# Small last blocks, loops over a place's blocks, and an earlier small-block table in the MoE section of a one-core kernel

## The chip, the cores and the metric

The kernel runs on one core of a Trainium2 chip. The metric is the time of one execution on the device in microseconds (us); lower is better. A core has TensorE (PE, matrix products; loading of the stationary operand is shown apart as PEld), VectorE (DVE), ScalarE (ACT), GpSimd (POOL) and the queue engine SyncE (SP), which here starts the large transfers. Each engine works through its own list of instructions in order and waits for others through semaphores. Matrix products collect in PSUM, whose banks DVE and ACT read.

## The reference

One layer: a mixer (HGRN2 heads and a convolution), a norm, then a mixture of 16 SwiGLU experts with two experts for each of 512 tokens, and a norm. The part around the change is the mixture:

```python
s = jax.nn.sigmoid((t @ router_w).astype(jnp.float32))       # 512 tokens x 16 experts
...
_, idx = lax.top_k(jnp.where(in_group, sb, -jnp.inf), TOP_K)  # best 2 in the best group
...
for e in range(N_EXPERTS):
    h = jax.nn.silu(t @ w_gate[e]) * (t @ w_up[e])            # 1024 -> 512
    y = y + combine[:, e:e + 1] * (h @ w_down[e])             # 512 -> 1024
```

How many tokens an expert gets is known only on the chip. The router's tables are worked out there: for each expert how many tokens it has, and for each row of work which token it takes and with which weight.

## The kernel before, in words

The execution has three parts: the mixer (up to about 322 us), a prologue that works out the router's tables and the first block, and a section written by hand (`moe`, from about 353 us), in which each engine has a program of its own with loops, branches on registers and semaphores.

**Places and blocks.** The experts are worked through in 16 "places": the first three are experts 0, 1 and 2, whose weights are loaded early; the others follow by their number of tokens in a fixed pattern. With the reference's inputs the places hold 9 (raised to 33), 42, 23, 1, 343, 49, 16, 38, 15, 257, 12, 31, 165, 22, 1 and 0 tokens. A place is cut into blocks of up to 64 rows, 26 in all. A **large** block takes 64 rows by 512 columns in two column groups of PE; a **small** one, for a place of at most 32 rows, takes 32 rows by 256 columns in four, with half the time on PE. Before, a place is small or large as a whole. Places 2, 3, 6, 8, 10, 11, 13 and 14 are small.

**Weights.** SP keeps a ring of weights for three places: eight tiles of gate and up, four of down. PE's `mark("fg", 8)` tells SP that a place's gate and up tiles have all been used and may be loaded over, `mark("fd", 4)` the same for down. SP then starts the transfers for the place three further on, and each pair of tiles raises a semaphore `full_g`, the down tiles `full_d`.

**One block in the section.** PE waits for `e` (a buffer is free) and `x` (the block's rows, turned and modulated, are in XT). It does the gate and up products of the eight chunks k = 0 to 7 (`up`, L501), with two transposes of the block before between k = 3 and 4 (`turn`, L599). Then it transposes the rows of the next block (`turned_rows`, L492), waits for `h`, and does the down product of the block **before** (`down`, L510). Meanwhile ACT applies Silu (L692) and copies the gathered rows (L685); DVE copies the turned hidden rows (L719, which gives `h`), multiplies (L724), modulates the next block's rows into XT (L727 and L729, which gives `x`) and evicts the product with its weights (L739). POOL gathers rows by index (L487) and adds results into DRAM (L832). Which size DVE and POOL use for a block is read from a table `cnt` (columns 64 on) which `small` fills.

**A place on PE.** `place(x)` does the first block (`block_`, of the size of the place, with waits for the weights), then `finish(x - 1)`, the down product of the last block of the place before, then marks `fd`, and then `rest`, a loop over the blocks from the second on, all large. Then it marks `fg`. The section begins with two register loads of counts (`load`), `rest(0)`, and then a loop of 15 places, three in a turn.

**The prologue.** `tables` (L293 on) works out indices and weights between the chunks of the first block's up product (`between(i)` issues the chunks that `todo[i]` lists). `small` (L220) comes behind the first block's Silu (L531) and multiplication (L532); then the second block's rows are turned and modulated (L346, L347). The first block's results sit in two banks of their own (`pg`, `pt`). Two ACT operations (L525) write ones into the banks `pz[0]` and `pz[1]` beforehand, and a dummy Silu (L527) asks for the Silu's table early. The order in which instructions stand on an engine here is set by a scheduler from their dependences.

Line 1002 in the profile is a helper that records all operations of the mixer. Line 103 is the router's first step on DVE; L131 and L158 are matmuls of its choice of experts and of the gathering of the first rows.

Of the kernel before, what the change touches and what calls it, by code (L numbers as in the profile page):

```python
# [85 lines left out]
class Router:  # L86
# [85 lines left out]
    def order(self, bank):  # L172
# [44 lines left out]
        self.bs, self.nrows = work.tile([16, 1]), rows  # L217
        v.tensor_copy(self.bs, ps[0:16, 80:81])

    def small(self, bank):  # L220
# [7 lines left out]
        v.tensor_scalar(at, K.iotab[:16, :], self.bs, sm[:, 1:2], op0=OP.is_equal, op1=OP.mult)  # L228
        ps = bank()
        nc.tensor.matmul(ps[0:1, 0:32], K.onesb[:16, 0:1], at, start=True, stop=True, skip_group_check=True)  # L230
        v.tensor_copy(K.cnt[:, 64:96], ps[0:1, 0:32])
# [60 lines left out]
    def tables(self, bank, between):  # L292
# [5 lines left out]
        pi, p32 = pb[:, 0:32], pb[:, 32:64]  # L298
# [21 lines left out]
    def weight_tables(self, bank, between):  # L320
# [11 lines left out]
        between(1)  # L332
# [5 lines left out]
        between(2)  # L338
# [130 lines left out]
def moe(nc, tc, K, ctx, work, W, n2d, zd, out):  # L469
# [11 lines left out]
    pg = psum.tile([128, 2, 256], F32, name="pg", bufs=1)  # L481
    pt = psum.tile([128, 4, 2, 64], F32, name="pt", bufs=1)
# [32 lines left out]
    todo = {0: (0, 1, 2, 3, 4, 5), 1: (6,), 2: (7,)}  # L515
# [5 lines left out]
    bank = lambda: psum.tile([128, 512], F32, name="tbl", bufs=2)  # L521
    with tc.manual_schedule():

        for p in (pz[0][:, 0, :], pz[1][:, 0, :]):
            s.activation(p.rearrange("p (a n) -> p a n", a=4), K.onesb[:, None, :].to_broadcast([128, 4, 128]), AF.Copy)  # L525
# [7 lines left out]
        K.router.small(bank)  # L533
        turned_rows()
        modulate(v, K, st.XT, pt)
# [3 lines left out]
    pg = pz[2][:, 0, :].rearrange("p (u n) -> p u n", u=2)  # L539
    pt = pz[2][:, 1, :].rearrange("p (c h r) -> p c h r", c=4, h=2)  # L540
    ph, po = pz[3][:, 0, :], pz[3][:, 1, :]
# [43 lines left out]
    with tc.tile_critical():  # L585
        with nc.Block() as block:  # L586
            @block.tensor
            def _(pe):
                pe.sem_inc(sem["e"], 1)
                pe.sem_inc(sem["x"], 1)  # L590
# [11 lines left out]
                def block_(x, n, fresh, nxt=None):  # L602

                    for k in range(8):
                        if k == 4:
                            turn()
                        if fresh and k % 2 == 0:
                            wait(pe, full_g[x % 3][k // 2], 64)
                        if k == 6 and nxt:
                            nxt()  # L610
# [13 lines left out]
                def rest(x):  # L624

                    with pe.If_lt(rows[x % 3], 65):
                        pass
                    with pe.Else():
                        with pe.Fori(64, rows[x % 3], 64):
                            take(pe, "e")  # L630
                            take(pe, "x")
                            block_(x, 2, False)
                            take(pe, "h")
                            product(x, 2)
                    mark("fg", 8)

                def by_rows(x, f):
                    with pe.If_lt(rows[x % 3], 33):
                        f(1)
                    with pe.Else():  # L640
                        f(2)

                def finish(x):
                    take(pe, "h")
                    by_rows(x, lambda n: product(x, n))

                def place(x, nxt):

                    take(pe, "e")
                    take(pe, "x")  # L650
                    by_rows(x, lambda n: block_(x, n, True, nxt))
                    finish(x - 1)
# [1362 lines left out]
```

## Time and profile before

| what | value |
|---|---|
| median of 3 runs | 672.32 us (672.11 to 676.18) |
| the profiled execution's own time | 670.53 us |
| its span in the trace | 668.7 us |
| mean granted clock of TensorE | 0.930 of full speed |
| PE busy | 576.2 us, 86% of the span |
| DVE / ACT / POOL busy | 343.1 / 168.1 / 254.3 us |
| moved by DMA | 170.66 MB, mean 255 GB/s |

The profile is one execution. A row of a timeline gives the start in us from the span's beginning, the length in us, the engine, the line of the code, the operation, the tiles written and read, and how many instructions the row holds; a bracket at its end gives the idle time of the engine just before, and what ended it ("PEq L554" is PE's own sequencer waiting for a semaphore in the section). [...] The DMA share is the mean busy share of the core's 16 DMA engines.

### The profile page before, as it was taken

To read this page: it belongs to the slowest core of one execution; us is meant where nothing else is said; L and a number is where in the kernel's file an instruction comes from. 1 tells how busy PE (TensorE), PEld (TensorE's weight loads), DVE (VectorE), ACT (ScalarE), POOL (GpSimd) and SP (SyncE) were. 2 spreads that over 40 slices of the span, in tenths; PEclk is the share of its full clock that TensorE was granted. 3 is DMA by queue.
4 is the path that set the end of the run, shared out by engine and by line. 5 is a ranking of instruction groups with operands and counts; after the bars stand their busy time and mean duration, and the time that the engine had idled before them with its cause. 6 is when DMAs were issued, how large, how long until landed. Compare 5 with 4: busy or idle time off the path is not lost. (4 is left out here: it accounts for less than half of the span.)

```text
span 668.7 us, 10479 instructions
## 1 busy us (share of the span) xinstructions
PE 576.2 (86%) x3499; PEld 313.9 (47%) x3500; DVE 343.1 (51%) x693; ACT 168.1 (25%) x256; POOL 254.3 (38%) x209
## 2 busy tenths in 40 slices
PE   4899999897997968996776979999976999999970
PEld 2577878565665535774432423333332333433430
DVE  6547596999669774788651312231321222322355
ACT  1443468534411233318110000000100101101112
POOL 2235594977921332647202222213221121331315
PEclk9999999897778978997977989999989999999976
DMA  8963322696336778739985999924999995799943
GB/s 293 353 209 98 97 91 67 218 306 243 92 117 217 255 275 303 256 136 395 378 259 193 368 375 390 374 69 117 374 376 383 387 383 163 250 377 376 319 148 126
DMA packets 78783, 170.66 MB, mean 255 GB/s; under 512 B 8866, under 2 KB 18031, under 8 KB 78718
## 3 DMA queue, kind: packets, MB, share of 16 engines
q1 hardware_dynamic: 69456, 149.19, 62.3%
q0 software_dynamic: 9136, 20.80, 11.4%
q8 instruction: 21, 0.34, 0.2%
q14 instruction: 28, 0.23, 0.1%
q10 hardware_dynamic: 142, 0.09, 0.0%
HBM read 154.96 MB, written 15.34 MB: 255 GB/s over the span
## 5 line engine op out<-in xcount | busy, mean ns | idle before, releaser
L832 POOL DMA_INDIRECT zd<-flat,dst x25 | 39.9, 1596 | 203.0 <-POOLq L554 189.1
L501 PE MATMUL pz<-wt,flat 128*32 128x256 f32 (+1 forms) x672 | 93.1, 490 | 5.7 <-PEq L554 5.7
L1002 POOL TENSOR_TENSOR wL<-w,wH 128x1024 fp32r<-128x1024 f32 x30 | 73.9, 2466 | 55.2 <-ACT wH L1002 55.1
L510 PE MATMUL pz<-wt,flat 128*64 128x512 f32 (+1 forms) x544 | 83.8, 513 | 3.1 <-PEq L554 2.0
L1002 PE MATMUL pj<-U,wH 128*128 128x512 f32 x256 | 80.6, 394 | 4.2 <-DVE U L1002 3.2
L1002 PE MATMUL pj<-wH,U 128*128 128x512 f32 x224 | 77.1, 416 | 7.0 <-DVE q L1002 4.6
L501 PE MATMUL pz<-R,flat 128*64 128x512 f32 (+1 forms) x384 | 67.9, 534 | 6.8 <-PEq L554 6.8
L692 ACT ACTIVATE flat<-pz 128x256 f32<-128x256 f32 x25 | 9.6, 383 | 238.6 <-ACTq L554 238.6
L1002 DVE SCALAR_TENSOR_TENSOR mx<-R,convw,mx 128x512 f32<-128x512 f32 x88 | 66.4, 754 | 3.4 <-DVEq L1891 0.6
L1002 PEld LDWEIGHTS pj<-wH,U 128*128 128x128 f32 x224 | 44.5, 199 | 26.7 <-issue 13.1
L501 PEld LDWEIGHTS pz<-wt,flat 128*32 128x32 f32 (+1 forms) x672 | 32.6, 124 | 50.2 <-issue 44.8
L724 DVE TENSOR_TENSOR flat<-pz,flat 128x256 f32<-128x256 f32 x25 | 10.6, 424 | 88.2 <-DVEq L554 82.2
L1002 PEld LDWEIGHTS pj<-U,wH 128*128 128x128 f32 x256 | 47.5, 188 | 16.7 <-DVE U L1002 4.4
L719 DVE COPY flat<-pz 128x256 f32<-128x256 f32 x26 | 11.0, 424 | 80.6 <-DVEq L554 72.3
L1002 PE MATMUL pj<-U,wL 128*128 128x512 f32 x128 | 49.9, 390 | 0.0
L510 PEld LDWEIGHTS pz<-wt,flat 128*64 128x64 f32 (+1 forms) x544 | 27.4, 128 | 44.5 <-issue 40.9
L1002 PE MATMUL pj<-wL,U 128*128 128x512 f32 x112 | 45.6, 407 | 0.0
L487 POOL DMA_INDIRECT flat<-n2d,idx_i x28 | 27.8, 991 | 42.4 <-issue 23.2
L501 PEld LDWEIGHTS pz<-R,flat 128*64 128x64 f32 (+1 forms) x384 | 22.3, 129 | 41.2 <-issue 39.3
L1002 POOL TENSOR_TENSOR R<-R 128x512 f32<-128x512 f32 x28 | 39.3, 1408 | 4.6 <-ACT R L1002 3.3
L1002 ACT ACTIVATE wH<-w 128x1024 fp32r<-128x1024 f32 x30 | 31.5, 1054 | 26.9 <-PE pj L1002 13.7
L739 DVE SCALAR_TENSOR_TENSOR flat<-pz,X,g2h 128x512 f32<-128x512 f32 x18 | 13.5, 751 | 38.5 <-DVEq L554 38.5
(394 smaller groups left out, 805.2 us busy)
## 6 DMA issues: line engine op xcount, KB each, us to landing
wt<-in_w_down_dram SPq DMA_DIRECT2D x60, 512.0 KB, 10.6
wt<-in_w_gate_dram SPq DMA_DIRECT2D x80, 256.0 KB
wt<-in_w_up_dram SPq DMA_DIRECT2D x80, 256.0 KB, 8.6
q<-in_ada_w_dram SPq DMA_DIRECT2D x28, 512.0 KB, 8.3
w<-in_w_in_dram SPq DMA_DIRECT2D x24, 512.0 KB, 3.8
aw<-in_ada_w_dram SPq DMA_DIRECT2D x20, 512.0 KB, 7.1
R<-in_w_gate_dram SPq DMA_DIRECT2D x40, 256.0 KB, 5.6
R<-in_w_up_dram SPq DMA_DIRECT2D x40, 256.0 KB, 7.9
```

The source lines that it names most:

```text
L487: return g.indirect_dma_start(out=to, out_offset=None, in_=n2h, in_offset=bass.IndirectOffsetOnAxis(ap=K.idx[:, i:i + 1], axis=0))
L501: i = eng.matmul(pg[m * j:m * j + m, :, 0:cw], xT[:, c, h, 0:m], w[:, :, cw * j:cw * j + cw], start=k == 0, stop=k == 7)
L510: i = eng.matmul(po[m * q:m * q + m, 0:dw], st.hT[:, c * 128 + j * m:c * 128 + j * m + m], W.dn(x, f)[:, dw * q:dw * q + dw], start=f == 0 ...
L692: s.activation(st.SL, pg[:, 0, :], AF.Silu).then_inc(sem["s"], 1)
L719: v.tensor_copy(st.hT, ph[:, 0:256]).then_inc(sem["h"], 1)
L724: v.tensor_tensor(st.HB, pg[:, 1, :], st.SL, op=OP.mult).then_inc(sem["e"], 1)
L739: v.scalar_tensor_tensor(st.o[j % 3][:, :256 * n], po[:, :256 * n], w[:, j:j + 1], g2, op0=OP.mult, op1=OP.mult).then_inc(sem["o"], 1)
L832: g.indirect_dma_start(out=zd.rearrange("r (q c) -> (r q) c", c=dw), out_offset=bass.IndirectOffsetOnAxis(ap=dst[:, j:j + 1], axis=0), in_ ...
L1002: return f(out, *a, **k)
```

## The change

1. `small` marks the **last block of each place** small if at most 32 rows are left in it, whatever the place's size. It moves from behind the first block's multiplication into `tables`, between the first two and the next four chunks of the first up product, and the matmuls that gather the tokens of 32-row blocks (L309) move ahead of the first chunks, into a bank of their own.
2. The second block's rows are modulated inside the section, as DVE's first work there, and PE no longer counts `x` up itself.
3. `pg`, `pt`, `ph` and `po` lie in the two last pairs of banks from the start; the two fills with ones (L525) are gone.
4. On PE a place is one loop over its blocks. In each turn a compare chooses a small or a large block, a second one whether the product is that of a block of the same place or the last one of the place before (`finish`, by a register `left` that holds how many rows were left). The waits for the gate and up tiles no longer count down; `done` does that, once a place, ahead of the mark `fg`. A third register load stands at the section's start.

With the inputs above the places whose last block becomes small are 4 (343 rows, the sixth block has 23) and 9 (257 rows, the fifth has 1).

The diff, cut to its core:

```diff
     def small(self, ps):
-        v.tensor_scalar(sm[:, 0:1], self.nrows, 0.0, None, op0=OP.is_gt)
-        v.scalar_tensor_tensor(sm[:, 1:2], self.nrows, 32.0, sm[:, 0:1], op0=OP.is_le, op1=OP.mult)
+        v.scalar_tensor_tensor(sm[:, 0:1], self.bs, 64.0, self.nb, op0=OP.subtract, op1=OP.add)
+        v.tensor_tensor(sm[:, 1:2], self.nrows, self.nb, op=OP.subtract)
+        v.tensor_scalar(sm[:, 1:2], sm[:, 1:2], -32.0, None, op0=OP.is_le)
...
+        v.tensor_scalar(at, K.iotab[:16, :], sm[:, 0:1], sm[:, 1:2], op0=OP.is_equal, op1=OP.mult)
+        nc.tensor.matmul(ps, K.onesb[:16, 0:1], at, start=True, stop=True, skip_group_check=True)
+        v.tensor_copy(K.cnt[:, 64:96], ps)
...
+        pb2 = bank()
+        pi, p32 = pb[:, 0:32], pb2[:, 32:64]
...
-        between(0)
         for i in range(8):
             for q in range(4):
                 nc.tensor.matmul(p32[32 * q:32 * q + 32, :], toks[:, i, 0:32], K.st.ones[:, i], start=i == 0, stop=i == 7,
                                  skip_group_check=True)
+        between(0)
+        self.small(pb2[0:1, 64:96])
+        between(1)
         self.weights()
...
-    todo = {0: (0, 1, 2, 3, 4, 5), 1: (6,), 2: (7,)}
+    todo = {0: (0, 1), 1: (2, 3, 4, 5), 2: (6,), 3: (7,)}
...
-        for p in (pz[0][:, 0, :], pz[1][:, 0, :]):
-            s.activation(p.rearrange("p (a n) -> p a n", a=4), K.onesb[:, None, :].to_broadcast([128, 4, 128]), AF.Copy)
         s.activation(st.SL[:, 0:1], K.rexp[:, 0:1], AF.Silu)
...
-        K.router.small(bank)
         turned_rows()
-        modulate(v, K, st.XT, pt)
...
+                def finish(x):
+                    take(pe, "h")
+                    with pe.If_lt(left, 33):
+                        product(x, 1)
+                    with pe.Else():
+                        product(x, 2)
+                def blocks_(x, first, nxt=None):
+                    n = rows[x % 3]
+                    with pe.Fori(first, n, 64) as at:
+                        take(pe, "e")
+                        take(pe, "x")
+                        with pe.If_lt(n, at + 33):
+                            block_(x, 1)
+                        with pe.Else():
+                            block_(x, 2)
...
+                            with pe.If(at > 0):
+                                again()
+                            with pe.Else():
+                                finish(x - 1)
+                                mark("fd", 4)
+                                wait(pe, full_d[x % 3], 64)
+                                nxt()
+                        pe.reg_alu(left, n, at, OP.subtract)
+                def done(x):
+                    for k in range(4):
+                        pe.sem_inc(full_g[x % 3][k], -64)
+                    mark("fg", 8)
...
+                pe.reg_load(left, K.cnt[0:1, 0:1])
...
+                modulated()
...
-                    for k in range(4 if i else 0):
+                    for k in range(4):
```

The places below are those at which the order of instructions on an engine differs. A row is a line, an operation, tiles, and a shape or a count.

**ACT, from the mixer's tail to the first block's Silu, before.** `X` and `q` are tiles of the norm that ends the mixer, `sg` are the router's sigmoids.

```order
L1002 ACTIVATE X<-X,zmv 128x1024
L1002 ACTIVATE q_84<-X,zmv 128x1024
...
L1002 ACTIVATE flat<-pj,cc 128x128 x2
L1002 ACTIVATE sg<-pj 128x16 x4
L165 ACTIVATE flat<-pj 128x512
L525 ACTIVATE pz_3142<-onesb 128x512
L525 ACTIVATE pz_3143<-onesb 128x512
L527 ACT_TABLE_LOAD
L527 ACTIVATE flat<-rexp 128x1
...
L531 ACTIVATE flat<-pg 128x256
```

The same stretch of ACT in the changed kernel (line 1020 is the helper's new number):

```order
L1020 ACTIVATE X<-X,zmv 128x1024
L528 ACT_TABLE_LOAD
L528 ACTIVATE flat<-rexp 128x1
L1020 ACTIVATE q_84<-X,zmv 128x1024
...
L1020 ACTIVATE flat<-pj,cc 128x128 x2
L1020 ACT_TABLE_LOAD
L1020 ACTIVATE sg<-pj 128x16 x4
L165 ACTIVATE flat<-pj 128x512
...
L532 ACT_TABLE_LOAD
L532 ACTIVATE flat<-pz_3142 128x256
```

The dummy Silu with its table load has moved up, behind the first `X` activation of the norm; the sigmoids and the first block's Silu each have a table load directly ahead of them, and the two fills are gone.

**DVE, the end of the prologue and the section's start, before.** The branches are the entry into the section.

```order
L331 COPY flat<-tbl 64x32
L532 TENSOR_TENSOR flat<-pg,flat 128x256
L225 TENSOR_SCALAR flat<-flat 16x1
L226 SCALAR_TENSOR_TENSOR flat<-flat 16x1
L228 TENSOR_SCALAR flat<-iotab,flat 16x32
L231 CAST cnt_i<-tbl 1x32
L346 TENSOR_TENSOR flat<-pt,scT 128x512
L347 TENSOR_TENSOR flat<-flat,shT 128x512
L2010 UNCONDITIONAL_BRANCH
L715 UNCONDITIONAL_BRANCH
```

The same stretch of DVE in the changed kernel:

```order
L334 COPY flat<-tbl 64x32
L533 TENSOR_TENSOR flat<-pz_3142,flat 128x256
L2028 UNCONDITIONAL_BRANCH
L728 UNCONDITIONAL_BRANCH
L731 TENSOR_TENSOR flat<-pz_3143,scT 128x512
L733 TENSOR_TENSOR flat<-flat,shT 128x512
L557 TENSOR_LOAD cnt_i
```

The four operations of `small` have left the prologue's end, and the two of the modulation stand behind the entry.

**PE, the end of a place's turn in the changed kernel.** L514 are down products, L614 are marks; the first compare chooses between a further block of the place and `finish`, the second the size of the last product of the place before.

```order
L635 UNCONDITIONAL_BRANCH
L644 COMPARE_AND_BRANCH
L514 MATMUL pz_3143<-wt_3080,flat 64x512 x2
...
L644 UNCONDITIONAL_BRANCH
L622 COMPARE_AND_BRANCH
L514 MATMUL pz_3143<-wt_3067,flat 32x256 x4
...
L614 MATMUL pz_3142<-onesb 32x1
L590 ISA
L590 TENSOR_LOAD cnt_i
L646 UNCONDITIONAL_BRANCH
L651 ISA
L630 COMPARE_AND_BRANCH
L614 MATMUL pz_3142<-onesb 32x1
```

Before, PE has there, for the loop over a place's blocks from the second on:

```order
L510 MATMUL pz_3143<-wt_3080,flat 64x512 x2
L510 MATMUL pz_3143<-wt_3081,flat 64x512 x2
L510 MATMUL pz_3143<-wt_3077,flat 64x512 x2
L510 MATMUL pz_3143<-wt_3078,flat 64x512 x2
L629 REGISTER_ALU
L629 COMPARE_AND_BRANCH
L628 UNCONDITIONAL_BRANCH
L621 MATMUL pz_3143<-onesb 32x1
```

Behind the product of a block two compares and the register load now stand, where only the loop's own compare stood.

## Rows read from the trace of the kernel before

**Rows 1.** Windows: busy us (instructions) by engine, granted clock, DMA share, GB/s.
```profile
440.00:461.00 21.00, 21.00 (x101) 6.85 (x96) 5.02 (x9) 2.03 (x4) 5.17 (x4) 1.00 0.27 50
491.00:524.00 33.00, 23.68 (x169) 8.97 (x164) 5.90 (x11) 2.03 (x4) 5.17 (x4) 0.84 1.05 388
...
570.00:635.00 65.00, 63.63 (x567) 26.34 (x565) 19.69 (x35) 7.09 (x14) 18.08 (x14) 1.00 0.98 339
...
637.00:638.00 1.00, 0.36 (x4) 0.21 (x8) 0.42 (x2) 0.00 (x0) 1.00 (x1) 0.50 0.00 0
```

**Rows 2.** Timeline of PE (start, length, line, tiles, count): place 4's last block.
```profile
449.27 3.60 PE L501 MATMUL pz<-wt,flat 128*64 128x512 f32 x16
...
457.34 3.65 PE L510 MATMUL pz<-wt,flat 128*64 128x512 f32 x16
```

**Rows 3.** Timeline of PE: blocks of places 9 to 12.
```profile
575.00 3.65 PE L510 MATMUL pz<-wt,flat 128*64 128x512 f32 x16
...
578.59 0.42 PE L501 MATMUL pz<-wt,flat 128*32 128x256 f32 x3
...
583.29 1.93 PE L510 MATMUL pz<-wt,flat 128*32 128x256 f32 x32
...
586.18 3.65 PE L501 MATMUL pz<-R,flat 128*64 128x512 f32 x16 [0.95 <-PEq L554]
...
596.45 3.65 PE L501 MATMUL pz<-R,flat 128*64 128x512 f32 x16 [0.21 <-PEq L554]
```

**Rows 4.** Timeline of DVE: the rows for place 12's first and second block.
```profile
584.92 0.69 DVE L729 TENSOR_TENSOR flat<-flat,shT 128x512 f32<-128x512 f32 x1
...
595.61 0.69 DVE L729 TENSOR_TENSOR flat<-flat,shT 128x512 f32<-128x512 f32 x1
```

**Rows 5.** Timeline of ACT, from the mixer's tail to the section.
```profile
302.47 1.28 ACT L1002 ACT_TABLE_LOAD   x1
303.76 0.20 ACT L1002 ACTIVATE early<-early 128x1 f32<-128x1 f32 x1
...
321.70 0.82 ACT L1002 ACTIVATE sg<-pj 128x16 f32<-128x16 f32 x4
...
338.28 1.28 ACT L527 ACT_TABLE_LOAD   x1
...
349.58 0.38 ACT L531 ACTIVATE flat<-pg 128x256 f32<-128x256 f32 x1 [0.76 <-PE pg L501]
```

**Rows 6.** Timeline of DVE, from the mixer's tail to the section.
```profile
315.82 0.81 DVE L1002 TENSOR_SCALAR q<-X,zmv 128x1024 f32<-128x1024 f32 x1
...
322.55 0.23 DVE L103 TENSOR_TENSOR flat<-sg,rbias 128x64 f32<-128x64 f32 x1 [1.73 <-ACT sg L1002]
...
350.00 0.42 DVE L532 TENSOR_TENSOR flat<-pg,flat 128x256 f32<-128x256 f32 x1 [2.31 <-ACT flat L531]
...
352.55 0.69 DVE L347 TENSOR_TENSOR flat<-flat,shT 128x512 f32<-128x512 f32 x1
```

**Rows 7.** Timeline of POOL in the mixer's tail.
```profile
314.97 0.19 POOL L1002 TENSOR_TENSOR zmv<-zmv 128x1 f32<-128x1 f32 x1
```

**Rows 8.** Timeline of PE, from the router to the section's first mark.
```profile
322.15 2.75 PE L1002 MATMUL pa<-onesb 128*128 128x512 bf16 x12
325.85 0.20 PE L131 MATMUL pj<-flat,tri 128*128 128x64 bf16 x1 [0.95 <-DVE flat L125]
...
327.31 1.94 PE L158 MATMUL pj<-q,flat 128*64 128x512 f32 x8 [0.92 <-DVE flat L152]
...
337.89 8.08 PE L501 MATMUL pg<-R,flat 128*64 128x512 f32 x24 [1.13 <-DVE flat L347]
...
356.42 0.18 PE L621 MATMUL pz<-onesb 128*32 128x1 bf16 x1 [4.64 <-PEq L554]
```

**Rows 9.** Timeline of PE: matmuls behind idle time in the section.
```profile
507.44 1.94 PE L501 MATMUL pz<-R,flat 128*64 128x512 f32 x8 [1.15 <-PEq L554]
...
637.64 3.24 PE L510 MATMUL pz<-wt,flat 128*32 128x256 f32 x32 [1.97 <-PEq L554]
```

More of the change, by code (lines that the diff above doesn't have):

```diff
@@ L216, in order, with small @@
         v.tensor_copy(K.cnt[:, 48:49], ps[0:1, 48:49])
-        self.bs, self.nrows = work.tile([16, 1]), rows
+        self.bs, self.nb, self.nrows = work.tile([16, 1]), nb, rows
         v.tensor_copy(self.bs, ps[0:16, 80:81])
-    def small(self, bank):
+    def small(self, ps):
         nc, K, work = self.nc, self.K, self.work
@@ L606, in block_ @@
                             turn()
[L607 to L610, printed above, removed]
+                        if k % 2 == 0:
+                            pe.wait_ge(full_g[x % 3][k // 2], 64)
                         i = up(pe, W.gu(x, k), st.XT, n, k)
@@ L622, in mark @@
                               skip_group_check=True).then_inc(sem[name], n)
-                def rest(x):
-                    with pe.If_lt(rows[x % 3], 65):
-                        pass
-                    with pe.Else():
[L629 to L632, printed above, removed]
+                left = pe.alloc_register("moe_left")
+                def finish(x):
+                    take(pe, "h")
+                    with pe.If_lt(left, 33):
+                        product(x, 1)
+                    with pe.Else():
+                        product(x, 2)
@@ L633, in rest, with again @@
+                def blocks_(x, first, nxt=None):
[7 more added lines that the diff above has]
+                            block_(x, 2)
+                        def again():
                             take(pe, "h")
                             product(x, 2)
-                    mark("fg", 8)
@@ L637, in by_rows @@
[L637 to L645, printed above, removed]
-                def place(x, nxt):
[L649 to L652, printed above, removed]
-                    mark("fd", 4)
-                    wait(pe, full_d[x % 3], 64)
-                    rest(x)
+                        if first:
+                            again()
+                        else:
+                            with pe.If(at > 0):
+                                again()
+                            with pe.Else():
[3 more added lines that the diff above has]
+                                nxt()
@@ L657, in _ @@
+                        pe.reg_alu(left, n, at, OP.subtract)
+                def done(x):
+                    for k in range(4):
+                        pe.sem_inc(full_g[x % 3][k], -64)
+                    mark("fg", 8)
+                def place(x, nxt):
+                    blocks_(x, 0, nxt)
+                    done(x)
                 load(0, 0)
                 load(1, 1)
+                pe.reg_alu(rows[2], rows[0], 0, OP.add)
+                pe.reg_load(left, K.cnt[0:1, 0:1])
                 wait(pe, full_d[0], 64)
-                rest(0)
+                with pe.If_lt(rows[0], 65):
+                    pass
@@ L661, in _ @@
+                with pe.Else():
+                    blocks_(0, 64)
+                done(0)
                 with pe.Fori(0, 15, 3) as at:
```

32 lines of the change are left out of this document (13 added, 19 removed).

## The prediction

> **What bounds the kernel now.** I read the table of windows first, because the bound changes along the section. While the last blocks of place 4 run, PE is busy for all of 21.00 us and the DMA stands at 0.27: the next weights wait for PE to release a slot. From 491 to 524 it is the reverse: DMA share 1.05, PE busy 23.68 of 33. From 570 on PE is the bound again, 63.63 of 65 us, at full clock [rows 1]. So a microsecond of PE saved at place 4 starts idle transfers a microsecond earlier, and one saved at place 9 or later shortens PE's own queue. The timelines of PE and DVE give the price of a block of each kind [rows 2 to 4]. Then, ahead of the section I followed the chain backwards: the router begins on DVE at 322.55, having waited 1.73 us for ACT's sigmoid; the first product ends behind 349.5; ACT's Silu and DVE's multiplication follow, then the small-block table and the modulation of the second block, until 353.24; PE's first mark in the section comes at 356.42 [rows 5, 6, 8].
>
> **The change part by part.** The sum is made against the profiled execution's own 670.53 us (span 668.7); the median of the three runs, 672.32, lies 1.79 higher, and the difference found is put on it.
>
> *Two more table loads, ahead of the router.* The listing of ACT's queue shows what the diff does not say: with the two fills of pz gone, the dummy Silu and its ACT_TABLE_LOAD are scheduled into the mixer's tail, so the sigmoids need a load of their own and the first real Silu a third. Now there is one load, at 338.28, while PE is in the first product and nothing waits for it. A load takes 1.28 us and the dummy behind it 0.20 [rows 5]. The first pair, 1.48, lands where ACT works without a gap; what depends on it runs over POOL, whose last small operation ends at 314.97 + 0.19 = 315.16, to DVE, which is free for it at 315.82 [rows 6, 7]. That is 0.66 of slack, so 0.8 comes through. The second load stands directly ahead of the sigmoids (321.70), for which DVE already waits: 1.28. Together **+2.1**.
>
> *The third load* stands ahead of the Silu at 349.58, which already waits 0.76 us for the product [rows 5]. The load sits behind the same wait: **+1.3**.
>
> *Small blocks and the modulation leave the prologue.* DVE's multiplication ends at 350.42, the modulation at 353.24 [rows 6]. These 2.82 us go, and about 0.1 more on PE for the token matmuls that move into a gap: **-2.9**. The small-block chain itself now lies beside chunks 0 and 1 of the first product, 2.7 of its 8.08 us for six chunks [rows 8]; that hides its steps on DVE, which are less than half of the 2.82. The weights behind it then end about when PE asks for them, so with that cover gone it would cost up to some 0.5. I take nothing. The second block's modulation is still done in time, while PE enters the section.
>
> *Entry.* From 353.24 to PE's mark at 356.42 lie 3.18 us with two register loads in them [rows 6, 8]. A third load and four semaphore decrements are added. If the 3.18 were loads alone, one would cost 1.6; if loads were pipelined, nothing. I take 0.5 + 0.15: **+0.65**. DMA is idle there, so this is on the path.
>
> *The clock.* The 2.1 us above also stretch PE's idle time ahead of L131 from 0.95 to some 2.2, since the matmuls before it (322.15, 2.75 long) are delayed by 0.8 only [rows 8]. [...]
>
> *Place 4's last block small.* The counts worked out from the reference's inputs are 343 tokens for place 4 (six blocks, the last of 23 rows) and 257 for place 9 (five, the last of 1 row); these two are the only blocks that become small. The eight that were small stay so. Up to the product a large block takes 449.27 to 457.34 = 8.07 [rows 2]; a small one 578.59 to 583.29 = 4.70 [rows 3]. The weights' slot is released 3.37 earlier while the DMA is nearly idle, and that lead is carried into the stretch where the DMA is the bound [rows 1]: **-3.4**. The smaller product saves PE another 3.65 - 1.93 = 1.7 in that place [rows 2, 3], which the DMA-bound stretch swallows.
>
> *Place 9's last block small* gives the same **-3.4**, here with PE as the bound. Its product is finished in place 10: large, 575.00 to 578.59 = 3.59; small, 583.29 to 586.18 = 2.89, since behind it PE waits for the next rows [rows 3]: **-0.7**.
>
> *Branches in the loops.* The compare that chooses a block's size now stands behind the wait for x, in every block. Without a compare, x ready at 595.61 + 0.69 = 596.30 is followed by PE at 596.45, 0.15 later; with one, 585.61 by 586.18, 0.57 [rows 3, 4]: 0.42 per compare that nothing covers. Behind a small product PE waits for x, so in the second blocks of places 4, 9 and 12 it shows: **+1.3**. Behind a large product x is ready early, and 575.00 to 578.59 already holds compares and marks without a loss [rows 3]; so I cost the other eight inner blocks at nothing (bound 8 x 0.42 = 3.4). The register load behind place 12's entry **+0.3** (0 to 0.5); the exit of the loop behind a small product **+0.6** (an estimate, one and a half of the 0.42); the second compare ahead of the products of places 10, 11, 13 and 14, mostly under the wait for h, **+0.3** (0 to 1.7).
>
> Sum: 2.1 + 1.3 - 2.9 + 0.65 + 0.9 - 3.4 - 3.4 - 0.7 + 1.3 + 0.3 + 0.6 + 0.3 = **-2.95**; 667.6 in a profiled execution, **669.4** on the median.
>
> **The rivals.**
> *A, faster.* If the added loads lie beside other work (the -3.4 of the two loads ahead of the router and at the Silu) and PE's clock holds (-0.9): 669.4 - 4.3 = 665.1. For it: ACT is idle for long stretches. Against: DVE's 1.73 us wait for ACT and the Silu's place directly behind the product [rows 5, 6]. 0.13.
>
> *B, slower than before.* PE's sequencer does not run ahead of the new compares. Then every inner block pays the 0.42 that is seen where nothing covers it: 8 x 0.42 = 3.4, and the first blocks of places 1 to 14 another 2.3 (14 x 0.16, some 0.4 of a compare, since part of them stands under a wait): 669.4 + 5.7 = 675.1. It decides from 2.95 / 8 = 0.37 per inner block. For it: the 0.57 at 586.18. Against: nothing is lost at 578.59. 0.15. [...]
>
> *C, place 4 gives nothing.* If the DMA-bound stretch ends when it does now whatever starts earlier, its -3.4 is lost: 672.8. Against: DMA at 0.27 before it [rows 1]. 0.06.
>
> *D, a switch of tables costs more than its load.* Were there a drain as long as the load behind each, the three loads would cost 3 x 1.28 = 3.8 more: 673.2. Against: the next ACTIVATE at 303.76 starts right at the load's end, 302.47 + 1.28, and the load right behind its forerunner [rows 5]. 0.04. [...]
>
> **How the numbers follow.** The likeliest case, 0.62, gives 669.4, its own range 667 to 671.5 by the open ends of clock, entry and branches. The range 664.9 to 673.0 takes in A and C, and leaves D and most of B out, 2 in 10 together. A measurement of this kernel can tell about 1% from no change, here 665.6 and 679.0. Faster by more: A alone, 0.13. Slower by more: B with the clock and entry at their upper ends, 0.04. Within 1%: 0.83.
>
> **What would show each step.** In the changed profile: ACT_TABLE_LOAD ahead of the sigmoids and of the first Silu, the router's first DVE row at about 324.6, the first product starting near 340 to 341; the Silu's end, not the modulation, as the last thing ahead of the section; nine of the narrow evictions (128x256) in the section's loop, in place of seven; place 4's first mark about 3 us earlier against the section's start, and the DMA-bound stretch with it; PE's first up of an inner block within 0.1 us of the product's end (else B); L158's eight matmuls at 1.94 or 3.9 us. I am wrong if PE idles in front of inner blocks, or if the loads do not appear in DVE's wait.

## The result, and the profile after

The changed kernel takes 667.36 us (median of 20 runs) against 671.38 for the kernel before. The ratio is 0.9934, 95% interval 0.9917 to 0.9951, some 4.4 us. The prediction was 669.4 on a median of 672.32, 0.9957. The profiled execution took 665.42 with a span of 663.6, against 670.53 and 668.7: 5.1 less. Some runs, the profiled run of e2_ln among them, had a lower clock over the whole span; the ratios here and below, and the comparisons of traces, leave them out.

A common scale for two traces is the table load in the mixer's tail, at 302.47 before [rows 5] and 301.90 after; this 0.57 is of the run, not of the change. From there the span divides so (the last column compares the stretch that ends at the row; place 11 and place 12 mean the start of their first matmuls):

| stretch, to | before at | after at | longer by |
|---|---|---|---|
| the table load in the mixer's tail | 302.47 | 301.90 | -0.57 |
| the router's first DVE row | 322.55 | 323.29 | +1.31 |
| DVE's multiplication | 350.00 | 350.01 | -0.73 |
| PE's first mark in the section | 356.42 | 356.61 | +0.18 |
| place 4: mark ahead of its second block | 402.59 | 404.57 | +1.79 |
| place 4: second block | 402.99 | 405.65 | +0.68 |
| place 4: last mark | 460.93 | 460.30 | -3.29 |
| place 9: mark ahead of its second block | 523.54 | 522.43 | -0.48 |
| place 9: second block | 523.93 | 523.53 | +0.71 |
| place 9: last mark | 570.31 | 566.62 | -3.29 |
| place 11 | 578.59 | 574.25 | -0.65 |
| place 12 | 586.18 | 582.15 | +0.31 |
| place 12: second block | 596.45 | 593.37 | +0.95 |
| the turn behind the loop | 635.26 | 632.67 | +0.49 |
| the end | 668.7 | 663.6 | -2.51 |

The rows of after that answer to [rows 5 and 6], the timelines of ACT and DVE (start, length, line, operation, tiles; the bracket is the idle time ahead and what ended it):

```profile
308.86 1.28 ACT L528 ACT_TABLE_LOAD   x1
310.15 0.20 ACT L528 ACTIVATE flat<-rexp 128x1 f32<-128x1 f32 x1
310.26 1.22 ACT L1020 ACTIVATE q<-X,zmv 128x1024 f32<-128x1024 f32 x1
...
321.55 1.28 ACT L1020 ACT_TABLE_LOAD   x1
322.84 0.41 ACT L1020 ACTIVATE sg<-pj 128x16 f32<-128x16 f32 x4
...
348.30 1.28 ACT L532 ACT_TABLE_LOAD   x1 [0.75 <-PE pz L505]
349.59 0.38 ACT L532 ACTIVATE flat<-pz 128x256 f32<-128x256 f32 x1
```

```profile
323.29 0.23 DVE L103 TENSOR_TENSOR flat<-sg,rbias 128x64 f32<-128x64 f32 x1 [2.73 <-ACT sg L1020]
...
350.01 0.42 DVE L533 TENSOR_TENSOR flat<-pz,flat 128x256 f32<-128x256 f32 x1 [3.85 <-ACT flat L532]
353.89 0.69 DVE L731 TENSOR_TENSOR flat<-pz,scT 128x512 f32<-128x512 f32 x1 [3.46 <-SPq L581]
```

The three loads are there, each 1.28 us. The first row to surprise is the last: the multiplication is done at 350.43, and DVE then waits 3.46 us for SP to let it into the section. PE's rows for [rows 8] and for the parts of [rows 1] that lie under the prologue:

```profile
326.60 0.20 PE L131 MATMUL pj<-flat,tri 128*128 128x64 bf16 x1 [1.97 <-DVE flat L125]
...
328.05 2.53 PE L158 MATMUL pj<-q,flat 128*64 128x512 f32 x8 [0.92 <-DVE flat L152]
...
338.61 1.94 PE L505 MATMUL pz<-R,flat 128*64 128x512 f32 x8
...
356.61 0.16 PE L614 MATMUL pz<-onesb 128*32 128x1 bf16 x1 [7.82 <-issue]
359.51 5.56 PE L505 MATMUL pz<-wt,flat 128*64 128x512 f32 x16 [2.73 <-issue]
```

Windows of the changed kernel (busy time of PE, PEld, DVE, ACT, POOL; granted clock; DMA share; GB/s):

```profile
328.00:336.00 8.00, 6.71 (x26) 1.76 (x26) 6.71 (x37) 0.59 (x1) 0.00 (x0) 0.58 1.09 326
338.00:344.00 6.00, 6.00 (x73) 2.21 (x71) 4.48 (x19) 0.00 (x0) 1.08 (x1) 1.00 1.03 332
```

PE's granted clock is 0.58 of full speed in the window under the router (0.50 from 330 to 336) and 1.00 in the first product, whose first eight matmuls take 1.94. Before, it was the other way round: 1.00 from 328 to 336, and 24 took 8.08 [rows 8] at 0.66 from 337.89 to 345.97. In the section, the last blocks of places 4 and 9, which are small now:

```profile
452.03 1.93 PE L505 MATMUL pz<-wt,flat 128*32 128x256 f32 x32
...
456.72 3.65 PE L514 MATMUL pz<-wt,flat 128*64 128x512 f32 x16
...
558.36 1.93 PE L505 MATMUL pz<-R,flat 128*32 128x256 f32 x32
...
563.04 3.65 PE L514 MATMUL pz<-wt,flat 128*64 128x512 f32 x16
```

Up to the product they take 4.69 and 4.68 us, where a large one took 8.07 [rows 2]. The rows for place 4's second block and for the end:

```profile
404.57 0.17 PE L614 MATMUL pz<-onesb 128*32 128x1 bf16 x1
405.65 3.65 PE L505 MATMUL pz<-wt,flat 128*64 128x512 f32 x16 [0.90 <-PEq L550]
...
632.67 0.41 PE L594 MATMUL pz<-ident,flat 128*128 128x128 f32 x2 [0.53 <-PEq L550]
634.43 1.94 PE L514 MATMUL pz<-wt,flat 128*32 128x256 f32 x32 [1.35 <-PEq L550]
```

The last product took 1.94, at a granted clock of 1.00, where it took 3.24 before [rows 9], at 0.58; more than half of the final -2.51 is this, the rest the matmuls behind it (0.6) and a shorter wait ahead of it (0.6). The 1.3 of the product can't be counted for the change. In the profile of e1_late (below), whose code is the same there and whose PE is idle as long ahead of it, the product takes 3.24 again:

```profile
634.78 3.24 PE L514 MATMUL pz<-wt,flat 128*32 128x256 f32 x32 [1.34 <-PEq L550]
```

### The profile page after: what moved, and what is told of

It reads as the page before. It is cut to its first block, busy times and chain, and to the rows that moved or that the text cites. A ratio compares the mean times of both kernels' runs of the same rounds, so it can differ in the third digit from the quotient of the medians.

```text
span 663.6 us, 10798 instructions
## 1 busy us (share of the span) xinstructions
PE 566.4 (85%) x3595; PEld 310.2 (47%) x3596; DVE 342.9 (52%) x694; ACT 169.2 (25%) x256; POOL 255.1 (38%) x209
## 5 line engine op out<-in xcount | busy, mean ns | idle before, releaser
L505 PE MATMUL pz<-wt,flat 128*32 128x256 f32 (+1 forms) x704 | 91.2, 481 | 9.0 <-PEq L550 3.3
L514 PE MATMUL pz<-wt,flat 128*32 128x256 f32 (+1 forms) x576 | 79.2, 484 | 1.3 <-PEq L550 1.3
L505 PE MATMUL pz<-R,flat 128*64 128x512 f32 (+1 forms) x448 | 72.2, 513 | 8.5 <-DMA R<-in_w_up_dram 4.8
L505 PEld LDWEIGHTS pz<-wt,flat 128*32 128x32 f32 (+1 forms) x704 | 31.6, 124 | 53.5 <-issue 43.2
L1020 PEld LDWEIGHTS pj<-U,wH 128*128 128x128 f32 x256 | 47.5, 188 | 16.3 <-DVE U L1020 4.4
L514 PEld LDWEIGHTS pz<-wt,flat 128*32 128x32 f32 (+1 forms) x576 | 26.8, 123 | 39.5 <-issue 34.4
L757 DVE SCALAR_TENSOR_TENSOR flat<-pz,X,g2h 128x512 f32<-128x512 f32 x16 | 12.0, 751 | 33.8 <-DVEq L550 33.8
```

The lines of the kernel that those rows point to most:

```text
L505: i = eng.matmul(pg[m * j:m * j + m, :, 0:cw], xT[:, c, h, 0:m], w[:, :, cw * j:cw * j + cw], start=k == 0, stop=k == 7)
L514: i = eng.matmul(po[m * q:m * q + m, 0:dw], st.hT[:, c * 128 + j * m:c * 128 + j * m + m], W.dn(x, f)[:, dw * q:dw * q + dw], start=f == 0 ...
L757: v.scalar_tensor_tensor(st.o[j % 3][:, :256 * n], po[:, :256 * n], w[:, j:j + 1], g2, op0=OP.mult, op1=OP.mult).then_inc(sem["o"], 1)
L1020: return f(out, *a, **k)
```

## The experiments

Every kernel is the changed one with the edit shown. The ratios are to the kernel before, with 95% intervals.

| kernel | ratio | interval |
|---|---|---|
| the changed kernel | 0.9934 | 0.9917 to 0.9951 |
| e1_late | 0.9953 | 0.9921 to 0.9986 |
| e2_ln | 0.9943 | 0.9905 to 0.9981 |
| e3_entry | 0.9939 | 0.9908 to 0.9970 |
| e4_large | 1.0059 | 1.0024 to 1.0094 |
| e5_takes | 0.9946 | 0.9922 to 0.9970 |
| e6_idle | 0.9986 | 0.9952 to 1.0020 |
| e7_ln_idle | 0.9947 | 0.9918 to 0.9976 |
| e8_all | 0.9873 | 0.9839 to 0.9907 |
| e11_best | 0.9842 | 0.9817 to 0.9867 |

### Sizes by place again

```diff
+        v.scalar_tensor_tensor(sm[:, 1:2], self.nrows, 32.0, sm[:, 1:2], op0=OP.is_le, op1=OP.mult)
-                        with pe.If_lt(n, at + 33):
+                        with pe.If_lt(n, 33):
-                        pe.reg_alu(left, n, at, OP.subtract)
+                        pe.reg_alu(left, n, 0, OP.add)
```

> The changed kernel with sizes chosen by place, as before: the last blocks of places 4 and 9 are large again; loops, order and everything else stay. By the prediction each is worth 3.4 and place 10's finish 0.7: 7.5 slower than the changed kernel, 1.004 of before. If place 4's gain is lost in the DMA-bound stretch (rival C): 4 slower, 0.999.

1.0059 against 0.9934 is 1.25%, 8.4 us. The prediction's 7.5 holds; rival C's 4 is out. The small last blocks carry the whole gain: without them the change is slower than the kernel before.

### The table loads taken off

```diff
-        s.activation(st.SL[:, 0:1], K.rexp[:, 0:1], AF.Silu)
+        s.activation(st.SL[:, 0:1], K.router.base[:, 0:1], AF.Silu)
```

> The changed kernel with one edit: the dummy Silu reads the router's block bases, so it and its table load stand behind the sigmoids again, and no load stands ahead of the sigmoids or of the first Silu. By the prediction's ledger the loads cost 2.1 + 1.3 = 3.4 us, so this should be 3.4 faster than the changed kernel: ratio to before about 0.988, section's first mark about 3 earlier. By the reading of the changed trace two things take it back: PE's idle time ahead of L131 shrinks from 1.97 to about 1, so the half-clock stretch falls under the first product again (24 matmuls in about 8 us, not 8 + 16 in 5.7), and SP's NOP at the section's entry waits for the ln2_b load until 352.9 in any case. Then the first mark moves by less than 1 and the ratio stays at 0.992 to 0.995.

No gain: 0.9953. The router starts 20.15 us behind the tail's table load (302.91 to 323.06; 20.08 before, 21.39 in the changed kernel), so the load ahead of the sigmoids did cost 1.3. But the half-clock stretch (the stretch in which PE is granted 0.50) is under the first product again; windows of e1_late:

```profile
328.00:336.00 8.00, 4.89 (x30) 1.74 (x28) 6.73 (x37) 0.80 (x2) 0.00 (x0) 1.00 1.08 326
338.00:344.00 6.00, 6.00 (x56) 1.83 (x54) 2.72 (x15) 0.00 (x0) 1.08 (x1) 0.50 1.04 323
```

The multiplication comes 27.31 us behind the router's first row (26.72 in the changed kernel, 27.45 before), although a load of 1.28 is gone: the clock took back 1.9.

### What the section's entry waits for

SP lets the engines into the section with a NOP; the question is what SP waits for ahead of it. The NOP in the changed kernel and in the kernel before, from the instructions of the entry's line:

```profile
L581 SPq NOP  x1: 18/18/18, 352.9 to 352.9; - x1
```

```profile
L585 SPq NOP  x1: 18/18/18, 353.6 to 353.6; - x1
```

Before, it followed the modulation (353.24) by 0.4. After, the multiplication is done at 350.43 and the NOP comes 2.5 later; the traffic of the last loads of the prologue, ln2_g and ln2_b, trickles on until 352, as the last two figures of these windows of the changed kernel show. Nothing needs them before the kernel's end.

```profile
351.00:352.00 1.00, 0.00 (x0) 0.00 (x0) 0.00 (x0) 0.00 (x0) 0.00 (x0) 1.00 0.11 45
352.00:353.00 1.00, 0.00 (x0) 0.00 (x0) 0.00 (x0) 0.00 (x0) 0.00 (x0) 1.00 0.00 0
```

```diff
-            nc.sync.dma_start(K.st.ln2g, bcast_rows(I["ln2_g"], D))
-            nc.sync.dma_start(K.st.ln2b, bcast_rows(I["ln2_b"], D))
+                    if x == 7:                      # in SP's program, ahead of take(sp, "fg", 8)
+                        sp.dma_start(K.st.ln2g, K.ln_rows[0]).then_inc(sem["ln"], 16)
+                        sp.dma_start(K.st.ln2b, K.ln_rows[1]).then_inc(sem["ln"], 16)
+                v.wait_ge(sem["ln"], 32)            # DVE, ahead of centred(0); POOL likewise
```

> The changed kernel with the loads of ln2_g and ln2_b moved into the section (SP starts them ahead of its wait for place 4's mark, where the DMA is idle). If SP's entry into the section waits for the trickling ln2_b load (NOP at 352.9, multiplication done at 350.43), the NOP moves to about 0.4 behind the multiplication, 2.0 earlier, and with it the first mark: ratio to before about 0.990. If the entry costs a fixed 2.5 us behind the last engine, whatever is loaded, the NOP stays and the ratio is 0.993.

The time says 0.9943, no gain. The NOP is read from e7_ln_idle, which has the same edit beside the late dummy Silu of e1_late and fewer warming matmuls (those that keep PE busy while the router starts, the first row of [rows 8]); e6_idle has these two alone.

```diff
-WARM = 12
+WARM = 8
```

> The kernel of e1_late with 8 instead of 12 of the matmuls that keep PE busy while the router starts, so PE idles about 1.9 us ahead of L131 again, without any table load. [...] The time: SP's entry still waits for the end of the loads, so 0 to 1 us faster than e1_late, ratio about 0.994.

> The kernel of e6_idle with the loads of ln2_g and ln2_b in the section as in e2_ln. If the end of these loads holds the section's entry, SP's NOP now follows the multiplication by 0.1 to 0.4 us and the first mark comes about 30 us after the router's first DVE row (33.3 in the changed kernel): with the 1.3 of the load ahead of the sigmoids, some 4.5 us faster than the changed kernel, ratio 0.986 to 0.988. If the entry waits for something else, ratio 0.992 or above.

The entry, DVE and SP of e7_ln_idle:

```profile
351.26 0.42 DVE L533 TENSOR_TENSOR flat<-pz,flat 128x256 f32<-128x256 f32 x1 [2.57 <-ACT flat L532]
352.83 0.69 DVE L731 TENSOR_TENSOR flat<-pz,scT 128x512 f32<-128x512 f32 x1 [1.15 <-SPq L581]
```

```profile
L581 SPq NOP  x1: 18/18/18, 351.8 to 351.8; - x1
```

DVE waits 1.15 instead of 3.46. From the multiplication's end to the NOP it is 0.1 us, and 3.0 in e6_idle, from which e7_ln_idle differs in these loads alone: the loads were what held the door. From the tail's table load to the NOP it is 51.1 us before, 51.0 in the changed kernel, 50.6 to 52.0 in the seven other profiles (e1_late, e3_entry to e6_idle, e9_warm16, e10_cold4) that load ln2 ahead of the section, whatever else they do in the prologue, and 47.5 to 49.0 in the three that don't (e7_ln_idle, e8_all, e11_best). So in the changed kernel no saving and no loss in the prologue under some 2.3 us reaches the section: not the small blocks and the modulation, not the third load, not the clock. The rest of the expectations failed. The 8 warming matmuls were to give PE its idle time ahead of L131 back (it is 1.83 in e6_idle, 1.82 in e7_ln_idle) and the first product its full clock by that. The first product was not freed: in e7_ln_idle the granted clock is 0.50 from 328 to 342, in e6_idle 0.82, 0.50 and 0.82 in the 2 us windows from 342 to 348, where the product's first eight matmuls take 3.13. And e6_idle, 0.9986, is slower if anything. And the earlier entry of e7_ln_idle is not seen in its time; see the last heading of this section.

### The clock

Two kernels with one run each, so without a ratio: the changed kernel with 16 warming matmuls, and e1_late with 4.

> The changed kernel with 16 instead of 12 warming matmuls: all three table loads stay, but PE's idle time ahead of L131 falls from 1.97 to about 1.0. If that idle time is what puts the half-clock stretch on the router's matmuls (328 to 336), it now falls under the first product, and the multiplication comes 28.7 us after the router's first DVE row instead of 26.7. If the idle time there has nothing to do with it, 26.7 stays.

> The kernel of e1_late with 4 instead of 12 warming matmuls: no load ahead of the sigmoids, PE idle about 2.8 us ahead of L131. If enough idle time there moves the half-clock stretch ahead of the first product, the multiplication comes 25.4 us after the router's first DVE row; with 8 matmuls (1.8 us idle) it was 27.3 to 28.3, so in between lies the point. If it is not the idle time, 27.3.

With 16, PE idles 1.09 ahead of L131 and the multiplication comes at 353.02, 28.70 behind the router's first row (324.32): the 2.0 us are gone, as the idle time would have it. Windows of e9_warm16, then of e10_cold4:

```profile
328.00:336.00 8.00, 6.42 (x30) 1.82 (x29) 6.51 (x40) 0.00 (x0) 0.00 (x0) 0.65 1.07 333
338.00:344.00 6.00, 5.22 (x60) 2.06 (x61) 2.89 (x12) 0.00 (x0) 1.08 (x1) 0.50 1.03 321
```

```profile
328.00:336.00 8.00, 6.48 (x30) 1.86 (x27) 5.85 (x35) 0.80 (x2) 0.00 (x0) 0.74 1.09 318
338.00:344.00 6.00, 5.61 (x63) 1.94 (x64) 3.00 (x14) 0.00 (x0) 1.08 (x1) 0.72 1.03 357
```

But 4 matmuls and 2.68 of idle time without the loads did not free the product: two half-clock stretches (granted 0.50 from 326 to 332 and from 340 to 342), and 27.92. The four profiles compared here of kernels with the three loads and 12 matmuls (the changed kernel, e3_entry, e4_large, e5_takes) show 26.71 to 26.73; none of the others does. What the clock goes by here is not settled. That 2 us of the first product go by it is shown (28.70 in e9_warm16, where the granted clock is 0.50 from 338 to 344, and 26.72 in the changed kernel, where it is 1.00); that these count for nothing as long as SP waits for the ln2 loads is shown by e9_warm16 too, whose multiplication is 2 us later and whose NOP is not (50.7 behind the tail's load).

### The entry's branch and the third register load

```diff
-                with pe.If_lt(rows[0], 65):
-                    pass
-                with pe.Else():
-                    blocks_(0, 64)
-                pe.reg_load(left, K.cnt[0:1, 0:1])
+                pe.reg_alu(left, rows[0], 0, OP.add)
```

> The changed kernel without the loop over place 0's further blocks on PE (place 0 has one block with these inputs, so nothing that runs is left out) and with left taken from rows[0] by a register operation, not a third load. If the branch at L633 that took 1.97 us at 357.5 waited for code to be fetched past the long body of place 0, the first up of place 1 follows its mark in about 0.9 us instead of 2.9; if such a branch costs that whatever stands before it, it stays at 2.9 or turns up at another first branch. The third load off: first mark 0.4 to 0.9 earlier. In time: place 3 waits for its weights anyway, so the 2 us come to nothing and only the mark counts: 0.4 to 0.9 faster than the changed kernel, ratio 0.992; if they were on the path, 2.9 faster, 0.989.

The compare that picks place 1's large block, on PE's sequencer: the changed kernel, then e3_entry (count, then shortest, median and longest in ns, and the start):

```profile
L633 PEldq COMPARE_BRANCH  x1: 1973/1973/1973, 357.5 to 357.5; - x1
```

```profile
L633 PEldq COMPARE_BRANCH  x1: 340/340/340, 358.6 to 358.6; - x1
```

Over the changed kernel's section the same line's median is 169 ns. This compare takes 1.97 us there and 0.34 in e3_entry: taking away code that never runs takes the time away. Before, where that loop holds a large block only, it was 0.22. The first up follows the first mark by 0.91 before, 2.90 after and 1.29 in e3_entry, by 2.8 to 3.5 in five other profiles with the loop (e5_takes to e7_ln_idle, e9_warm16, e10_cold4), and by 1.1 to 1.2 in the two others without it (e8_all, e11_best). The first large block stands behind that loop and the small variant. That the compare waits for this code, as the expectations of e3_entry and e8_all have it, was an estimate, which no row shows by itself; the edit takes the third load away too, whose register this compare doesn't read.

It is not the only compare that takes microseconds. The kernel before has one ahead of place 1's product, and the changed kernel a second one behind place 2's:

```profile
L638 PEldq COMPARE_BRANCH  x1: 2322/2322/2322, 374.1 to 374.1; - x1
```

```profile
L622 PEldq COMPARE_BRANCH  x1: 2388/2388/2388, 386.6 to 386.6; - x1
```

PE is idle 1.12 and 0.99 us there. In the other kernels the second one's idle time comes and goes: 0.92, 1.82 and 0.82 ahead of the same mark in e5_takes, e9_warm16 and e11_best, none in e6_idle to e8_all and e10_cold4.

From NOP to mark it is 3.7 in the changed kernel, 2.8 before, and 2.9 in e3_entry. The rows of PE's sequencer on this way in the changed kernel are the third load, the two compares of the loop that place 0 doesn't need, and the four semaphore decrements:

```profile
L666 PEldq TENSOR_LOAD <-cnt_i x1: 299/299/299, 355.1 to 355.1; - x1
L668 PEldq COMPARE_BRANCH  x2: 82/185/288, 355.6 to 355.7; - x2
L655 PEldq EVENT_SEMAPHORE  x4: 51/51/51, 356.1 to 356.5; - x4
```

By the starts of these rows in the trace the load takes 0.36 until the next instruction, a decrement 0.15. So the 0.9 over the kernel before are the load, 0.60 for the decrements and 0.10 for a register move, less 0.2 for the count of `x` that is gone; the 0.8 that e3_entry saves are the load and 0.49 for the compares.

In time, nothing: 0.9939. The rows where it goes, place 9's second block in e3_entry:

```profile
521.09 0.17 PE L614 MATMUL pz<-onesb 128*32 128x1 bf16 x1
523.75 5.35 PE L505 MATMUL pz<-R,flat 128*64 128x512 f32 x16 [2.48 <-PEq L550]
```

PE comes to the loop's wait for place 9's down tiles earlier, but its sequencer gets past that wait at 522.0, no sooner than in the changed kernel (521.7), and the first matmul follows 1.8 later in both. PE is idle for 2.48 us (0.92 after), and then does the first sixteen matmuls in 5.35 (3.65 after, at a granted clock of 1.00).

### The compare behind the wait

```diff
-                        take(pe, "e")
-                        take(pe, "x")
                         with pe.If_lt(n, at + 33):
+                            take(pe, "e")
+                            take(pe, "x")
                             block_(x, 1)
                         with pe.Else():
+                            take(pe, "e")
+                            take(pe, "x")
                             block_(x, 2)
```

> The changed kernel with the waits for e and x put into both branches, behind the compare that chooses the block's size. If the compare behind x is what the second blocks of places 4, 9 and 12 pay (0.9 us of idle time there, 0.2 before the change), it is now done while PE waits, and each gets 0.2 to 0.4 back, as do the first blocks behind a small product: 1 to 2 us in all, ratio to before about 0.991. If what is late there is the loop's end (the wait for the down tiles, the register load, the loop's own compare), nothing changes: 0.993.

At place 12 the second block follows the mark by 0.60 (593.30 to 593.90), by 1.34 in the changed kernel and 0.40 before. But most of this is not the compare's: e1_late, e9_warm16 and e10_cold4, which don't have the edit, have 0.81 there. At places 4 and 9 the step stays (1.20 and 2.56). What the edit saves is seen from the point at which PE's sequencer gets past the wait for the down tiles: 403.9, 521.7 and 591.6 in the changed kernel, 404.4, 521.7 and 592.3 in e5_takes. From there to the first matmul of the second block it takes 1.8 us in the changed kernel and 1.6 in e5_takes, at all three places. In these 1.8 stand the register load, the loop's compare, the waits for e and x, and the compare for the size; rows of PE's sequencer at place 4 in the changed kernel, and DVE's row that completes x there:

```profile
L550 PEldq EVENT_SEMAPHORE  x1: 51/51/51, 403.9 to 403.9; - x1
L590 PEldq TENSOR_LOAD <-cnt_i x1: 303/303/303, 404.2 to 404.2; - x1
L630 PEldq COMPARE_BRANCH  x1: 209/209/209, 404.6 to 404.6; - x1
L633 PEldq COMPARE_BRANCH  x1: 208/208/208, 405.4 to 405.4; - x1
```

```profile
404.13 0.69 DVE L733 TENSOR_TENSOR flat<-flat,shT 128x512 f32<-128x512 f32 x1
```

x is complete at 404.82, before the sequencer asks for it (405.1), so there is hardly a wait that could hide the compare. What is late is the end of the loop, as the expectation's other case has it; the edit gives 0.1 to 0.2 at each place, and no difference in time: 0.9946.

### All of it

> All of it together: late dummy Silu, 8 warming matmuls, ln2 loads in the section, no loop for place 0, left from a register, waits behind the compare. By adding what the traces showed: 4.5 from e7_ln_idle, 0.8 from the register load, up to 1.9 from the branch that waited for code, 0 to 2 from the waits: 5 to 9 us faster than the changed kernel, ratio 0.980 to 0.985. If the DMA-bound stretches give part of it back, only the entry's share stays: 0.988.

> The kernel of e8_all with the 12 warming matmuls of the changed kernel: late dummy Silu, ln2 loads in the section, no loop for place 0, left from a register, waits behind the compare. If the 8 matmuls did nothing for the clock, as the traces of e6 to e8 say, it is as fast as e8_all: ratio to before 0.985 to 0.990. If they did, it is 2 us slower, 0.990 to 0.992.

Together they are faster than both kernels: 0.9873 with 8 warming matmuls, 0.9842 with 12, which is 0.6 and 0.9% below the changed kernel's 0.9934. The 5 to 9 us expected of e8_all were 4, near the 0.988 of the entry's share alone. e11_best is not slower than e8_all, and in their profiles the multiplication comes 27.5 and 27.3 us behind the router's first row: the 8 matmuls did nothing for the clock. The entry of e11_best, NOP 0.1 behind the multiplication and place 1 1.1 behind the mark:

```profile
354.08 0.42 DVE L533 TENSOR_TENSOR flat<-pz,flat 128x256 f32<-128x256 f32 x1 [2.57 <-ACT flat L532]
355.65 0.69 DVE L729 TENSOR_TENSOR flat<-pz,scT 128x512 f32<-128x512 f32 x1 [1.14 <-SPq L581]
```

From the router's first row to the mark it is 33.9 before, 33.3 after, 30.9 in e11_best; from the mark to the end 312.3, 307.0 and 305.4. Where an earlier entry goes in the other kernels can be followed in their profiles: PE waits longer for the down tiles, and the matmuls behind that wait are slower: the sixteen that follow 2.37 to 2.65 us of idle time at place 9 in e3_entry, e5_takes, e7_ln_idle, e9_warm16 and e10_cold4 take 5.35, those behind 0.66 to 0.94 in the changed kernel, e8_all and e11_best 3.65. Place 9's second block follows its mark by 0.8 to 1.1 us in the changed kernel, e1_late, e8_all and e11_best, and the last mark comes 43.1 us later; it follows by 2.5 to 2.8 in e3_entry, e5_takes, e7_ln_idle, e9_warm16 and e10_cold4, and the last mark comes 44.8 later. Differences of 2 us drown in that. That this is why e2_ln, e3_entry and e7_ln_idle gained nothing alone is argued, not shown: each kernel has one profile.

## Why the prediction was right or wrong

**Place 4's and place 9's last blocks (-3.4 each), place 10's finish (-0.7): right.** -3.29, -3.29 and -0.65 in the trace; e4_large gives them all back, 8.4 with 7.5 expected.

**Interior blocks at nothing: right.** From place 4's second block on, a large block follows its forerunner as before (405.65 to 417.26 for a block and its product, 11.61; 402.99 to 414.60 before). Rival B asked for 0.37 a block.

**Compares in second blocks (+1.3): too low.** 0.68 + 0.71 + 0.95 = 2.34. The step took x for what PE waits for last there, and counted the compare behind it alone. In the changed kernel x is complete 0.8 to 1.1 us ahead of the first matmul (404.82, 522.52, 592.28); what ends last is the wait for the down tiles, with 1.8 us behind it for the register load, the loop's compare, two waits and the size's compare. The exit (+0.6) was +0.49, the second compare at place 11 +0.31 where 0.3 had been put on four places; at place 13 it is hidden.

**Table loads ahead of the router (+2.1): 1.31.** The second load came through as worked out, the first did not come through at all: the slack ahead of it was larger than the 0.66 that the one chain over POOL showed. **The third load (+1.3): right**, 1.28 between the product's end and the Silu. Of rival D, a drain behind each load, none of the three shows a trace: 310.15, 322.84 and 349.59 follow the loads of 1.28 us at once.

**The clock (+0.9): wrong in sign.** No run shows this term: it was an estimate, half of what L158's matmuls would lose if the idle time ahead of L131 halved the clock. The clock did fall there (granted 0.50 from 330 to 336; 2.53 and 3.68 for eight of these matmuls in place of 1.94), but the router's chain on DVE hid it, and the stretch that fell under the first product before, 24 matmuls in 8.08, was then at a granted clock of 1.00 (1.94 and 3.65 for 8 and 16): -2.0. That row stood in front of me, [rows 8]; 8.08 for 24, beside 1.94 for eight, should have been read as a half-clock price.

**The prologue's end (-2.9): wrong.** This is the step that failed most: "2.82 go" took DVE to be the last that the section waits for. From the multiplication's end to SP's NOP it was 3.2 before and is 2.5 now, so 0.7 of the 2.8 came; SP's wait for two loads that nobody needs yet took the other 2.1. The same wait swallows the third load and the clock: up to the section's entry the sum had +1.4, and -0.1 came (51.1 to 51.0 behind the tail's table load). That the error is no larger is luck.

**Entry (+0.65): mis-sized.** 0.9 from NOP to mark, the load nearly as taken (0.36 for 0.5) and the four decrements four times as dear (0.60 for 0.15). Behind the mark the compare of 1.97 cost 2.0, which no term held; the kernel before has one like it, the 2.32 us at 374.1, with PE idle for 1.12. At place 4 the profile is 1.8 later against the first mark; the clock (granted 0.50 from 392 to 396, and 0.50 and 0.85 in the halves of that window before), the second such compare (2.39) and a wait for tiles have their part in it.

**The end (no term): -2.51.** Some 1.9 of it is the clock in the last product (granted 1.00, before 0.58) and in the first matmuls behind it (0.74 from 638.64 to 641.20, before 0.59 from 643.18 to 646.38), and e1_late shows that the change doesn't bring it. It is as large as two thirds of the whole forecast, and it is luck. Why the wait ahead of the product is 0.6 shorter is open.

Between the two profiles the time behind the tail's table load fell by 4.5 us, where the sum has 2.95. Its terms for the small blocks, -7.5, came as -7.2, and that is no luck. The others missed in both directions: +1.8 up to place 4, +0.7 in the second blocks (2.3 for 1.3 and the 0.3 of a register load) and +0.2 at the entry stand against -1.5 up to the entry, -0.5 ahead of place 9 and -2.5 at the end. That these nearly cancel is luck.

## What to carry to other kernels

Before putting a price on work that leaves the end of a stage, list everything that the next stage's entry waits for, transfers that nobody needs yet among them: the second-latest bounds the gain. A removed instruction can free a scheduler to move others; compare the engines' orders, not the diff. Look at the sequencer's rows for a compare that takes microseconds (1.97 and 2.39 here), in the kernel before too (2.32). And ask of each wait what the sequencer still has to do behind it: at place 4 a load of 0.30 and two compares of 0.21 stood in the 1.8 us between the wait that ended last and the first matmul.

## What the runs showed of the hardware

A compare-and-branch on PE's sequencer took 0.07 to 0.34 us in the section, but for one of 2.32 in the kernel before and two of 1.97 and 2.39 in the changed kernel; the first of these two was 0.34 in e3_entry, without the loop for place 0. A register load took 0.30 to 0.53 us in the changed kernel, and the third one 0.36 until the next instruction at the entry; a semaphore decrement there 0.15. A table load took 1.28, and the next activation began at its end (310.15, 322.84 and 349.59 in the changed kernel). SP's NOP came 2.5 us behind the last computation in the changed kernel, where two loads were under way until 352, and 0.1 to 0.6 behind it in the three kernels that start them later. A stretch at a granted clock of 0.50 came in every profile compared between the router and the end of the first product; from the router's first row to the multiplication it was 26.72 in the changed kernel and 28.70 in e9_warm16 with the same loads, by where the stretch fell, and from 4 to 16 warming matmuls it could be moved but not steered. Behind 1.35 and 1.34 us of idle time the section's last product took 1.94, at a granted clock of 1.00, in the changed kernel and 3.24 in e1_late.
